# The border of two layers: layer 1's first weights split ahead of the residuals, the last group's tiles ended one by one, the root table loaded early

## Chip, cores and metric

The kernel runs on one core of a Trainium2 chip. A core has five engines with queues of their own that work side by side: TensorE (PE: matrix products, into PSUM), VectorE (DVE), ScalarE (ACT), GpSimd (POOL) and SyncE (SP, which here only issues loads). Each engine takes its instructions strictly in the order in which they were put in its queue, and waits at an instruction whose inputs are not there. The metric is the device time of one execution in microseconds (us), as the median of several.

## What is computed

Two layers of a diffusion backbone over 512 latent tokens with 256 context tokens, model width 1024, in fp32. Each layer is an attention block and a SwiGLU block, both with a modulated RMS norm ahead and a gated residual behind. Layer 0 mixes latent attention heads and neighbourhood heads, layer 1 has sliding-window heads. What matters here is the end of layer 0 and the start of layer 1:

```python
def swiglu(h, w_gate_up, w_down):
    g, u = jnp.split(h @ w_gate_up, 2, axis=-1)
    return (jax.nn.silu(g) * u) @ w_down

def modulate(x, shift, scale):
    return rms_norm(x) * (1 + scale) + shift
...
        h_lat = h_lat + g_f * swiglu(modulate(h_lat, sh_f, sc_f), ffn_w_gate_up[l], ffn_w_down[l])
        if ctx_out:
            h_ctx = h_ctx + cg_a * o_ctx
            h_ctx = h_ctx + cg_f * swiglu(modulate(h_ctx, csh_f, csc_f), ffn_w_gate_up[l], ffn_w_down[l])
...
def odd_mixer(a_lat, a_ctx, rows, cols, w_in, sinks, w_out, ctx_out):
...
    q, k, v = split(a_lat @ w_in, s)
```

So layer 1's first product (`a_lat @ w_in`) needs the norm of the whole residual stream, a sum of squares over all 1024 features of each token.

## The kernel before

**Numbers.** An fp32 operand is held as two parts, a rounded part and the rest, and a product is three matmuls (rounded by rounded, rounded by rest, rest by rounded; lines 320 to 322 in `mm3`, 1302 to 1304 in `product`). Splitting a loaded weight is a cast on ScalarE and a subtraction on VectorE: `load_w` (lines 307 and 308) for a 128x1024 weight panel, `parts` (lines 1289 and 1290) elsewhere. In the names of the trace, `wr` is a raw weight, `wh` and `wl`, `ph` and `pl`, or two tiles of `st` are its parts, `pss`, `pst`, `psd`, `pso` are PSUM banks (three, two, two and one of them). Activations stand with features on the partitions: eight feature tiles of 128, each with 512 latent columns (`LATS`) and 256 context columns (`CTXS`).

**The feed-forward.** `ffn` goes over the 22 inner tiles in groups (`CHUNKS`); layer 0's last group has the tiles 19, 20 and 21. Each is a `Pair` (gate and up tile at once, by a scheme of seven half-size products in place of eight): `head` (two products of 12 matmuls, "11" and "21"), `body` (T2, T3, T1), `tail` (22, T4), each on 384 columns. Between the products that share a bank, ScalarE copies the partial result out (lines 1341, 1348, 1351), and T1 cannot start before the copy of line 1348. The tail of a pair is written after the head of the next one. Its result is the product's second operand `hs`, in two halves of 384 columns, each a multiply (line 1360) and a split (lines 1289, 1290). Within a group the inner tiles are the contraction steps of the down product.

**The border.** After the last group `final0` adds the down product to the residual stream, tile by tile: `tile` (nine matmuls: three contraction steps of three), `residual` (VectorE, line 1166, then a square on ScalarE, line 1464), `add` (VectorE, line 1470: the running sum of squares). Seven latent tiles are written first; while they go, three weight panels of layer 1 (`first_w`: panels 8, 9, 0 of `w_in1`) are loaded and split. Then come the eighth latent tile, the context tiles (`C`, `RC`), and `normed`: 16 token sums on TensorE (line 1439), the root on ScalarE (line 1444), a reciprocal and four transposes. After that layer 1's products (`panels`) begin, between the remaining context tiles.

**What sets the order.** A scheduler orders each engine's instructions by data, by the order of the program and by a timeline of its own. Inside `in_order(...)` an engine keeps the program's order: before, that holds for VectorE from the first latent tile on, and for TensorE from the eighth on. Loads are issued by SP in one queue, each when its buffer is free; `wr` has three buffers, `nb` two, `rope` one. The `rope` buffer here takes the modulation weights of layer 1, one 512 KB load after the other, each used by one VectorE operation (line 215) and then replaced. The residuals of earlier groups lie in DRAM (`home`) and are fetched by POOL's queue.

Of the kernel before, what the change touches and what calls it, by code (L numbers as in the profile page):

```python
# [100 lines left out]
def hybrid_kernel(ctx: ExitStack, tc, I, out):  # L101
# [31 lines left out]
    def dma(o, i):  # L133
        return nc.sync.dma_start(f(o), f(i))
# [1039 lines left out]

    def kept_w(src, m):

        r = T("wr", [P, 384])
        dma(r, src(m))
# [127 lines left out]
    class Pair:  # L1306
# [38 lines left out]
        def body(self):  # L1345
# [3 lines left out]
            product(self.y, self.s3, self.ops["T3"], True)  # L1349
            product(self.z, self.s1, self.ops["T1"])  # L1350
# [3 lines left out]
        def tail(self):  # L1354
            product(self.z, self.s4, self.ops["22"])
# [3 lines left out]
            for c in (self.c2, self.c1) if self.w > NX else (slice(0, 2 * self.w),):  # L1359
                V.tensor_tensor(self.s[:, c], self.s[:, c], self.t[:, c], op=ALU.mult)  # L1360
                parts(self.s[:, c], *(x[:, c] for x in self.dst))

# [30 lines left out]
    def ffn(l, ops, sums, cs, tags, more, down, final):  # L1393

        for ci, (k0, kc) in enumerate(CHUNKS[l]):
            hs, last = [], None
            for j in range(k0, k0 + kc):
# [3 lines left out]
                elif j >= DIRECT[l]:  # L1401
# [4 lines left out]
                    if last:  # L1406
                        last.tail()
                    p.body()
# [14 lines left out]
    new = []  # L1423
# [22 lines left out]

    def final0(src, hs):
# [3 lines left out]
        ws = [ahead[0]] + [kept_w(src, m) for m in range(1, KT)]  # L1451
        sq, acc, ts, r = {}, {}, {}, {}
        more = (I["w_in1"][8], I["w_in1"][9], I["w_in1"][0])

        def tile(m, c, v):
            o = PG()
            o = o[:, : c.stop - c.start]
            mm3([(o, c)], ws[m], hs)
            return o
# [41 lines left out]
        def C(m):  # L1501
            ctx[m] = tile(m, CTXS, 1)
# [249 lines left out]
```

## Time and profile before

| what | us |
|---|---|
| median of three runs | 1618.03 |
| the three runs | 1613.65, 1618.28, 1618.03 |
| the profiled execution | 1612.09 |
| its span, first to last instruction | 1610.3 |
| TensorE busy in it | 1539.6 |
| VectorE busy in it | 1182.0 |
| mean granted TensorE clock | 0.986 |

A row of the trace's timeline is: start, duration, engine, line, operation, written tile <- read tiles, form, count; in brackets stands the engine's idle time before it and what ended it. A row of waits has the waiting engine, what it waited for, total, number of times and the longest. A row of stretches has the bounds, the length, then for PE, PE's weight loads, DVE, ACT and POOL the busy time (and number of instructions), the granted clock (1.00 is full), the DMA's busy share and GB/s. A row of a queue has packets, megabytes and its share; one of a load has its queue, the count, the size and the us from issue to landing. One feed-forward group of layer 0 ends, and the border lies, between about 940 and 1040 us of the span.

### The profile page before, as it was taken

The page shows a single profiled execution, that of the slowest core. Times are in us where ns is not written, and L with a number is a line of the kernel's source. Part 1 is how long each engine was busy: PE and PEld are TensorE (multiplying, and loading weights), DVE is VectorE, ACT ScalarE, POOL GpSimd, SP SyncE. Part 2 cuts the span into 40 slices and gives each one's busy share as a digit, 9 for nine tenths or more (in the row PEclk, how much of TensorE's full clock was granted, in tenths as well). Part 3 has the DMA queues.
Part 4 walks back from the last instruction along what each step waited for, and adds up shares of the span by engine and source line. Part 5 has one row for each costly group of instructions (what it writes and reads, how often), then busy time and mean ns, then how long its engine had stood idle before and what let it go on. Part 6 is the DMA issues. An engine that isn't in the chain of part 4 may idle for free.

```text
span 1610.3 us, 26632 instructions
## 1 busy us (share of the span) xinstructions
PE 1539.6 (96%) x10004; PEld 1375.9 (85%) x10004; DVE 1182.0 (73%) x2367; ACT 806.0 (50%) x1637; POOL 226.7 (14%) x219
## 2 busy tenths in 40 slices
PE   6999989999998999999999998999999999999997
PEld 4686877887988999998989997877889898899996
DVE  5495977577579687785867776768877688687686
ACT  5364587776455333342423244457756554454453
POOL 0152723230000000100000010283003000000000
PEclk9999999999998999999999999999999999999998
DMA  9445342004541465647565766121006133333322
GB/s 341 161 149 190 108 132 80 23 7 159 179 161 59 158 204 169 214 127 246 159 202 196 243 212 210 41 89 66 2 6 200 33 112 124 91 98 118 91 97 84
DMA packets 80465, 214.92 MB, mean 133 GB/s; under 512 B 10192, under 2 KB 17872, under 8 KB 80336
## 3 DMA queue, kind: packets, MB, share of 16 engines
q1 hardware_dynamic: 73552, 188.05, 36.5%
q0 software_dynamic: 4480, 22.02, 3.7%
q10 hardware_dynamic: 2304, 3.15, 0.5%
q8 instruction: 78, 1.28, 0.3%
q14 instruction: 51, 0.42, 0.1%
HBM read 186.97 MB, written 23.07 MB: 130 GB/s over the span
## 4 chain that ended last, share of the span: by engine, by line
PE 73%; DVE 12%; DMA 9%; issue 3%; ACT 2%; POOL 1%; SPq 0%; DVEq 0%; ACTq 0%
PE pso L532 5%; DMA rope<-in_mod_w_dram 4%; PE pss L320 4%; PE pss L321 4%; PE pss L322 4%; PE psd L320 3%; PE psd L321 3%; PE psd L322 3%; PE pss L1302 3%; PE pss L1304 3%; PE pss L1303 3%; PE psd L1304 3%; PE psd L1302 3%; PE psd L1303 3%; PE pst L479 2%
## 5 line engine op out<-in xcount | busy, mean ns | idle before, releaser
L307 ACT CAST wh<-wr 128x512 fp32r<-128x512 f32 (+2 forms) x142 | 108.4, 778 | 202.9 <-PE pss L321 43.3
L308 DVE TENSOR_TENSOR wl<-wr,wh 128x1024 fp32r<-128x1024 f32 (+2 forms) x139 | 127.1, 921 | 78.6 <-ACT wh L307 77.9
L538 ACT ACTIVATE p<-p,sm 128x512 f32<-128x512 f32 (+3 forms) x144 | 105.0, 730 | 26.3 <-DVE sm L542 24.0
L215 DVE CUSTOM_DVE_ANT_0 p<-rope,cond 128x1024 bf16<-128x1024 f32 x64 | 77.0, 1220 | 40.3 <-DMA rope<-in_mod_w_dram 40.1
L321 PE MATMUL psd<-b,wh 128*128 128x256 f32 (+4 forms) x257 | 87.7, 341 | 2.2 <-DVE b L1290 2.2
L1303 PE MATMUL pss<-b,wh 128*128 128x384 f32 (+1 forms) x270 | 84.0, 311 | 1.2 <-DVE b L345 1.2
L1302 PE MATMUL pss<-b,wh 128*128 128x384 f32 (+1 forms) x270 | 84.1, 311 | 0.7 <-ACT b L344 0.7
L1430 POOL DMA_DIRECT2D home<-p x40 | 21.6, 541 | 447.5 <-DVE p L1166 320.5
L1304 PE MATMUL pss<-b,wl 128*128 128x384 f32 (+1 forms) x270 | 83.9, 311 | 0.0
L320 PE MATMUL psd<-b,wh 128*128 128x512 f32 (+4 forms) x217 | 77.8, 358 | 2.1 <-ACT b L430 1.3
L320 PE MATMUL pss<-st,wh 128*128 128x256 f32 (+2 forms) x231 | 78.1, 339 | 0.4 <-ACT wh L307 0.4
L322 PE MATMUL pss<-st,wl 128*128 128x512 f32 (+2 forms) x231 | 77.8, 337 | 0.0
L532 PE MATMUL pso<-ph,b 128*64 128x256 f32 (+1 forms) x384 | 77.3, 359 | 0.3 <-DVE ph L470 0.2
L532 PE MATMUL pso<-pl,b 128*64 128x256 f32 (+1 forms) x384 | 76.8, 359 | 0.7 <-DVE pl L470 0.7
L322 PE MATMUL psd<-b,wl 128*128 128x512 f32 (+4 forms) x217 | 76.0, 351 | 0.0
L1304 PE MATMUL pst<-b,wl 128*128 128x384 f32 (+1 forms) x240 | 74.1, 310 | 0.6 <-DVE wl L1290 0.6
L1302 PE MATMUL pst<-b,wh 128*128 128x384 f32 (+1 forms) x240 | 74.5, 310 | 0.0
L1303 PE MATMUL pst<-b,wh 128*128 128x384 f32 (+1 forms) x240 | 74.5, 310 | 0.0
L321 PE MATMUL pss<-b,wh 128*128 128x256 f32 (+4 forms) x227 | 74.0, 327 | 0.1
L1289 ACT CAST wh<-ph 128x512 fp32r<-128x512 f32 x80 | 46.3, 620 | 43.8 <-PE pst L1303 14.6
L1302 PE MATMUL psd<-b,wh 128*128 128x384 f32 (+1 forms) x210 | 65.8, 313 | 0.0
L1304 PE MATMUL psd<-b,wl 128*128 128x384 f32 (+1 forms) x210 | 65.3, 313 | 0.5 <-DVE wl L1290 0.5
(606 smaller groups left out, 5385.0 us busy)
## 6 DMA issues: line engine op xcount, KB each, us to landing
wr<-in_w_gu_dram SPq DMA_DIRECT2D x88, 512.0 KB, 4.1
rope<-in_mod_w_dram SPq DMA_DIRECT2D x48, 512.0 KB, 3.5
wr<-in_w_out_dram SPq DMA_DIRECT2D x32, 512.0 KB, 3.6
wr<-in_w_dn_dram SPq DMA_DIRECT2D x64, 256.0 KB, 2.8
p<-home SPq DMA_DIRECT2D x40, 384.0 KB, 4.8
home<-p POOLq DMA_DIRECT2D x40, 384.0 KB, 4.5
wr<-in_w_in_dram SPq DMA_DIRECT2D x21, 512.0 KB, 4.0
st<-in_mod_wp_dram SPq DMA_DIRECT2D x32, 256.0 KB, 4.9
```

Source lines behind the costliest of these rows:

```text
L215: V.tensor_tensor_reduce(out=T("p", [P, D], mybir.dt.bfloat16), in0=w, in1=cond[:, v, :], op0=ALU.mult, op1=ALU.add, scale=1.0, scalar=0.0 ...
L307: S.copy(h, r)
L308: (G if eng else V).tensor_tensor(lo, r, f(h), op=ALU.subtract)
L320: PE.matmul(o, wh[:, k], mh[:, c], start=first and k == 0, stop=False)
L321: PE.matmul(o, wh[:, k], ml[:, c], start=False, stop=False)
L322: PE.matmul(o, wl[:, k], mh[:, c], start=False, stop=last and k == n - 1)
L532: ins = PE.matmul(o[64 * i : 64 * i + 64, c], v(kt), t, start=n == 0, stop=n == len(moving[i]) - 1)
L538: S.activation(p[:, c], p[:, c], AF.Exp, bias=nm, scale=-1.0, accum_out=dn)
L1289: S.copy(h, t)
L1302: PE.matmul(o, wh, xh, start=first and k == 0, stop=False, skip_group_check=not first)
L1303: PE.matmul(o, wh, xl, start=False, stop=False, skip_group_check=not first)
L1304: PE.matmul(o, wl, xh, start=False, stop=k == 3, skip_group_check=not first)
```

## The change

It touches the last group of layer 0's feed-forward and the border.

- The generator `ended` splits the last-but-one pair's tail in two, and `begin_border`, started at the last pair's head, fixes the order on TensorE and ScalarE from there (TensorE's until the border is done, ScalarE's until the last tail). It splits the down weights of tiles 0 and 1 and the layer 1 panel 8, starts tiles 0 and 1 on the first two contraction steps, then splits panel 9, and after the last tail panel 0.
- `final0` starts tiles 2, 3 and 4 on two steps as well (`started`), then all eight latent tiles go in order: tiles 0 to 4 need their third step only, 5 to 7 all three. All residuals come after the three splits of layer 1's weights.
- The raw down weights of tiles 2 to 7 go to the `nb` buffers, two to a buffer, in place of `wr`.
- A root of one column, whose result nothing reads, stands on ScalarE before the first residual; with it ScalarE's table for roots is loaded there.

```diff
+        if m < 2:
+            r = T("wr", [P, 384])
+        elif m % 2 == 0:
+            r = T("nb", [P, 768])
+            raw_w[:] = [r[:, 384:]]
+            r = r[:, :384]
+        else:
+            r = raw_w[0]
+        dma(r, src(m))
...
             product(self.y, self.s3, self.ops["T3"], True)
+            next(between, None)
             product(self.z, self.s1, self.ops["T1"])
...
-                    if last:
+                    if l == 0 and j == NFF - 1:
+                        between = begin_border(last, lambda m: I["w_dn"][l, m, :, k0 * P : (k0 + kc) * P], hs)
+                        next(between)
+                    elif last:
                         last.tail()
-                    p.body()
+                    p.body(between)
...
-            ahead.clear()
-            ahead[0] = kept_w(src, 0) if l == 0 and final and ci == len(CHUNKS[l]) - 1 else load_w(src(0), kc, P)
+            if l or ci < len(CHUNKS[l]) - 1:
+                ahead.clear()
+                ahead[0] = load_w(src(0), kc, P)
+            elif last:
+                next(between)
             if last:
                 last.tail()
+            next(between, None)
+            casts.close()
...
+    def lat_tile(m, w, hs, ks=(0, 3), o=None):
+
+        k = slice(*ks)
+        o = PG() if o is None else o
+        mm3([(o, LATS)], [x[:, k] for x in w], hs[k], ks[0] == 0, ks[1] == 3)
+        return o
+
+    def begin_border(last, src, hs):
+
+        fixed.enter_context(in_order(ON_PE))
+        casts.enter_context(in_order(ON_ACT))
+        tail = last.ended()
+        next(tail)
+        yield
+        for _ in tail:
+            pass
+        ahead.clear()
+        for m in range(2):
+            ahead[m] = kept_w(src, m)
+        first_w.append(load_w(I["w_in1"][8], KT, P))
+        yield
+        started.extend(lat_tile(m, ahead[m], hs, (0, 2)) for m in range(2))
+        first_w.append(load_w(I["w_in1"][9], KT, P))
+        yield
+        first_w.append(load_w(I["w_in1"][0], KT, P))
...
-        with in_order(ON_DVE):
-            for m in range(KT - 1):
-                residual(m, tile(m, LATS, 0), LATS, 0)
-                if m:
-                    add(m - 1, 0)
-                if m in (2, 4, 6):
-                    first_w.append(load_w(more[len(first_w)], KT, P))
-            with in_order(ON_PE):
-                residual(7, tile(7, LATS, 0), LATS, 0)
-                add(6, 0)
+        S.activation(T("sm", [P, 6, 2])[:, :1, 0], f(hs[2][0][:, :1]), AF.Sqrt, bias=eps, scale=0.0)
+        with fixed, in_order(ON_DVE):
+                started.extend(lat_tile(m, ws[m], hs, (0, 2)) for m in range(2, 5))
+                for m in range(KT):
+                    residual(m, lat_tile(m, ws[m], hs, *(((2, 3), started[m]) if m < 5 else ())), LATS, 0)
+                    if m:
+                        add(m - 1, 0)
```

How the instructions stand in the queues, at three places. A row has the line, the operation, the written tile <- the tiles read, and the shape. Line numbers of the changed kernel are higher, since lines were added.

VectorE, from the last split of the last pair's result on, before (line 308 is the split of a layer 1 panel, line 1166 a residual, line 1470 a sum of squares):

```order
L1290 TENSOR_TENSOR b_9695<-p_9728,b_9694 128x384
L1166 SCALAR_TENSOR_TENSOR b_9869<-psd_9931,mod_390_1879,b_9877 128x512
L1166 SCALAR_TENSOR_TENSOR b_9870<-pst_9944,mod_390_1879,b_9879 128x512
L1166 SCALAR_TENSOR_TENSOR b_9871<-pss_9957,mod_390_1879,b_9881 128x512
L1470 TENSOR_TENSOR p_9942<-p_9942,p_9955 128x512
L308 TENSOR_TENSOR wl_9974<-wr_9971,wh_9973 128x1024
L1166 SCALAR_TENSOR_TENSOR b_9872<-psd_9977,mod_390_1879,b_9883 128x512
L1470 TENSOR_TENSOR p_9942<-p_9942,p_9968 128x512
```

and now, from one row earlier in the same place:

```order
L1374 TENSOR_TENSOR p_9728<-p_9728,p_9729 128x384
L1299 TENSOR_TENSOR b_9695<-p_9728,b_9694 128x384
L308 TENSOR_TENSOR wl_9908<-wr_9905,wh_9907 128x1024
L1166 SCALAR_TENSOR_TENSOR b_9912<-psd_9853,mod_390_1879,b_9920 128x512
L1166 SCALAR_TENSOR_TENSOR b_9913<-pst_9860,mod_390_1879,b_9922 128x512
L1166 SCALAR_TENSOR_TENSOR b_9914<-pss_9967,mod_390_1879,b_9924 128x512
```

The third split of a layer 1 panel stands ahead of the first residual; the other two stand further ahead, between the steps of the last pair, and none is left among the residuals.

SP's queue, at the end of the last group, before (`wr` from `in_w_dn` is a raw down weight of 192 KB, `rope` from `in_mod_w` a modulation weight of 512 KB):

```order
L134 DMA rope_1935_9685<-in_mod_w_dram 128x1024
L134 DMA wr_9893<-in_w_dn_dram 128x384
L134 DMA wr_9899<-in_w_dn_dram 128x384
L134 DMA rope_1937_9689<-in_mod_w_dram 128x1024
L134 DMA rope_2076_10372<-in_rope_dram 128x1024
L134 DMA wr_9904<-in_w_dn_dram 128x384
```

and now:

```order
L134 DMA rope_1935_9685<-in_mod_w_dram 128x1024
L134 DMA wr_9829<-in_w_dn_dram 128x384
L134 DMA wr_9833<-in_w_in_dram 128x1024
L134 DMA rope_1937_9689<-in_mod_w_dram 128x1024
L134 DMA rope_2074_10374<-in_rope_dram 128x1024
L134 DMA wr_9867<-in_w_in_dram 128x1024
L134 DMA wr_9905<-in_w_in_dram 128x1024
```

The load just ahead of the last modulation weight is now layer 1's panel 8, of 512 KB, where a down weight of 192 KB stood.

ScalarE, around the last pair's products, now (line 1357 is the copy that T1 waits for, line 1361 the one that the product 22 waits for, line 1370 the activation behind 22):

```order
L1357 COPY p_9729<-pss_9730 128x384
L1298 CAST st_9544<-p_9578 128x384
L1298 CAST ph_9821<-wr_9823 128x384
L1298 CAST ph_9827<-wr_9829 128x384
L307 CAST wh_9835<-wr_9833 128x1024
L1298 CAST st_9936<-nb_9937 128x384
L1298 CAST st_9941<-nb_9937 128x384
L1298 CAST st_9945<-nb_9946 128x384
L1298 CAST st_9950<-nb_9946 128x384
L1361 COPY p_9729<-pss_9730 128x384
L307 CAST wh_9869<-wr_9867 128x1024
L1370 ACTIVATE p_9728<-pss_9730 128x384
```

and before:

```order
L1289 CAST st_9544<-p_9578 128x384 x2
L1348 COPY p_9729<-pss_9730 128x384
L1289 CAST st_9901<-wr_9899 128x384
L1289 CAST st_9906<-wr_9904 128x384
L1289 CAST st_9911<-wr_9909 128x384
L1351 COPY p_9729<-pss_9730 128x384
L1289 CAST st_9916<-wr_9914 128x384
L307 CAST wh_9973<-wr_9971 128x1024
L1356 ACTIVATE p_9728<-pss_9730 128x384
```

T1's copy now stands one cast of the pair before earlier, and between it and the copy of the product 22 stand all of the casts of six down weights and of the first layer 1 panel.

More of the change, by code (lines that the diff above doesn't have):

```diff
@@ L1173, in hybrid_kernel @@
     ahead = {}
+    raw_w = []
     def kept_w(src, m):
[L1177 to L1178 removed]
         if m < 2:
@@ L1354, in tail, with ended @@
         def tail(self):
+            for _ in self.ended():
+                pass
+        def ended(self):
             product(self.z, self.s4, self.ops["22"])
@@ L1395, in ffn @@
         for ci, (k0, kc) in enumerate(CHUNKS[l]):
-            hs, last = [], None
+            hs, last, between = [], None, iter(())
             for j in range(k0, k0 + kc):
@@ L1421, in ffn @@
                 final(src, hs)
-    new = []
+    new, fixed, casts = [], ExitStack(), ExitStack()
     def down0(m, w, hs):
@@ L1450, in final0, with tile @@
         old = [fetched(m, slice(0, NT), "b") for m in range(KT)]
-        ws = [ahead[0]] + [kept_w(src, m) for m in range(1, KT)]
+        ws = [ahead[m] if m < 2 else kept_w(src, m) for m in range(KT)]
         sq, acc, ts, r = {}, {}, {}, {}
[L1453 to L1458, printed above, removed]
+        def tile(m):
+            o = PG()[:, :NX]
+            mm3([(o, CTXS)], ws[m], hs)
             return o
@@ L1501, in C @@
         def C(m):
-            ctx[m] = tile(m, CTXS, 1)
+            ctx[m] = tile(m)
         def RC(m):
```

5 lines of the change are left out of this document (4 added, 1 removed).

## The prediction

> **What bounds the kernel now.** I read the page first, then TensorE's waits around the border of the layers, then that stage as a table of stretches, then the rows of single instructions.
>
> ```profile
> PE 1539.6 (96%) x10004; PEld 1375.9 (85%) x10004; DVE 1182.0 (73%) x2367; ACT 806.0 (50%) x1637; POOL 226.7 (14%) x219
> ...
> PE psd L1439 <- DVE p L1470: 5.6, 1, 5.6
> PE psd L320 <- ACT st L1289: 1.7, 1, 1.7
> ...
> 998.76:1004.32 5.56, 0.00 (x1) 0.00 (x0) 5.56 (x9) 1.82 (x3) 0.00 (x0) 0.72 0.92 280
> 1004.32:1010.53 6.21, 6.21 (x30) 6.21 (x30) 0.91 (x3) 2.43 (x5) 0.00 (x0) 0.50 0.48 143
> 1010.53:1016.37 5.84, 5.84 (x48) 5.84 (x47) 5.46 (x11) 3.09 (x6) 0.00 (x0) 0.92 0.00 0
> 1016.37:1036.00 19.63, 19.63 (x100) 16.36 (x98) 17.16 (x37) 10.56 (x20) 1.15 (x1) 1.00 0.00 1
> ```
>
> TensorE is busy for 96% of the span, so only what lets it wait, or slows its clock, has a price. The border has one large wait: for 5.56 us TensorE does nothing while VectorE is full (5.56 of 5.56). It costs twice, for in the next 6.21 us the granted clock is 0.50, and it is back at 1.00 only in the stretch after 1016.37. Which VectorE work is late, its rows say:
>
> ```profile
> 991.76 0.75 DVE L1166 SCALAR_TENSOR_TENSOR b<-psd,mod,b 128x512 f32<-128x512 f32 x1 [2.11 <-PE psd L322]
> ...
> 994.48 1.22 DVE L308 TENSOR_TENSOR wl<-wr,wh 128x1024 fp32r<-128x1024 f32 x1
> ...
> 1001.79 1.22 DVE L308 TENSOR_TENSOR wl<-wr,wh 128x1024 fp32r<-128x1024 f32 x1
> ...
> 1003.59 0.68 DVE L1470 TENSOR_TENSOR p<-p,p 128x512 f32<-128x512 f32 x1
> ```
>
> From the first residual (991.76) to the last sum (1004.27) VectorE has hardly a gap, and three of its operations are splits of layer 1's weights (the first and the last are shown, 1.22 each). At its pace, a little under the durations, they take 3 x 1.14 = 3.4 us, a residual 0.66 and a sum 0.60. TensorE had its last matmul before the wait at 998.48, after a border in this order:
>
> ```profile
> 983.28 0.34 PE L1302 MATMUL pss<-st,ph 128*128 128x384 f32 x1
> ...
> 985.38 0.39 PE L320 MATMUL pst<-st,st 128*128 128x512 f32 x1
> ...
> 994.36 0.39 PE L320 MATMUL psd<-st,st 128*128 128x512 f32 x1
> ...
> 996.45 0.29 PE L320 MATMUL pst<-st,ph 128*128 128x256 f32 x1
> ...
> 998.48 0.28 PE L322 MATMUL pss<-b,pl 128*128 128x256 f32 x1
> ```
>
> These rows give the three paces: 12 matmuls of 384 columns in 2.10 us (0.175 each), nine of 512 in 2.09 (0.232), 18 of 256 from 996.45 to 998.60 (0.119).
>
> **The change, part by part.**
>
> *Splits ahead of the residuals.* The changed order has all three before the first residual, so the chain from there is 8 residuals at 0.66 and 6 sums at 0.60, 8.9 us in place of 12.5. TensorE's own list is no shorter: tail product and last product of the final pair (24 x 0.175 = 4.2), first two contraction steps of tiles 2 to 4 (18 matmuls), third step of tiles 0 to 4 (15), tiles 5 to 7 (27), which is 60 x 0.231 = 13.9, two context tiles (2.1): 20.2 us. Tiles 5 to 7 now end one by one, so VectorE has caught up when tile 7 ends, as the context tiles begin. Residual 7 (0.66) and the sum behind it (0.60, with ScalarE's square beside it) take some 1.5 us with the hand-overs, the context tiles 2.1: the token sums' inputs come about 0.5 us early, and TensorE has no wait there. The 5.72 us from 998.60 to 1004.32 go; next late is TensorE itself.
>
> *The half clock goes with the wait.* At full clock the same operations stand later in the trace:
>
> ```profile
> 1024.76 0.95 PE L1439 MATMUL pss<-ones,p 128*128 128x1 f32 x8
> 1025.57 0.48 PE L758 MATMUL psd<-b,wh 128*128 128x512 f32 x1
> ...
> 1027.74 0.38 PE L449 MATMUL pso<-ident_r,sm 128*128 128x128 f32 x2
> 1027.88 0.47 PE L758 MATMUL psd<-b,wh 128*128 128x512 f32 x1
> ```
>
> Eight sums took 0.81, so 16 take 1.62; a context tile 9 x 0.119 = 1.07; four transposes 0.28. That is 2.97 for the stretch that took 6.21: 3.24 saved. The five context tiles behind it take 45 x 0.119 = 5.35 in place of 5.84: 0.49. Together 5.72 + 3.24 + 0.49 = **9.45 us** if TensorE comes to the context tiles when it did before.
>
> *Does it come there in time?* The last pair's product T1 now stands ahead of the first down tiles, and it needs the ScalarE copy of the product before it.
>
> ```profile
> 968.26 1.22 DVE L215 CUSTOM_DVE_ANT_0 p<-rope,cond 128x1024 bf16<-128x1024 f32 x1 [3.97 <-DMA rope<-in_mod_w_dram]
> ...
> 971.16 1.02 DVE L1290 TENSOR_TENSOR pl<-wr,ph 128x384 fp32r<-128x384 f32 x2
> ...
> 974.29 0.51 ACT L1289 CAST st<-p 128x384 fp32r<-128x384 f32 x1 [1.09 <-DVE p L1360]
> 974.71 0.47 ACT L1348 COPY p<-pss 128x384 f32<-128x384 f32 x1
> ...
> 974.85 0.50 PE L320 MATMUL psd<-st,ph 128*128 128x512 f32 x1 [1.67 <-ACT st L1289]
> ...
> 975.97 1.34 ACT L1289 CAST st<-wr 128x384 fp32r<-128x384 f32 x3 [0.79 <-PE pss L1303]
> ...
> 990.32 1.05 ACT L307 CAST wh<-wr 128x1024 fp32r<-128x1024 f32 x1 [1.26 <-DMA wr<-in_w_in_dram]
> ```
>
> The two splits at 971.16 move behind the tail of the pair before, so the multiply of that tail starts there; it takes 0.47, as each of them, the cast behind it 0.42, the copy 0.47, with 0.2 between engines: T1 starts at 972.7. Before, TensorE went idle at 974.85 - 1.67 = 973.18, and six matmuls of 512 columns (1.4) that then came first now stand behind T1: it is free at about 971.7. T1 ends at 974.8, and the 12 down matmuls at 977.6. The next product needs a copy that stands on ScalarE behind a tail's last cast (from 973.75, by the same paces), two casts, the weight's cast (1.05) and four casts (0.45 each): 978.25. From 978.35, 20.2 us end at 998.55, against 998.60 before. The old 1.67 us wait is traded for two smaller ones: zero, taken as between -1 and +1 us.
>
> *The load that gets in front.* All of this hangs on 968.26, where VectorE ended a 3.97 us wait for a 512 KB load. On SP's queue a 192 KB load went just before it; now a 512 KB load of layer 1's weight stands there.
>
> ```profile
> q0 software_dynamic: 362, 1.83, 64.1%
> q1 hardware_dynamic: 288, 0.72, 27.0%
> ...
> b<-home POOLq DMA_DIRECT2D x6, 384.0 KB, 6.7
> rope<-in_mod_w_dram SPq DMA_DIRECT2D x1, 512.0 KB, 5.8
> ...
> rope<-in_mod_w_dram SPq DMA_DIRECT2D x1, 512.0 KB, 3.4
> ...
> 967.00:968.00 1.00, 1.00 (x8) 1.00 (x7) 0.00 (x0) 0.00 (x0) 0.00 (x0) 1.00 1.05 434
> ...
> wr<-in_w_in_dram SPq DMA_DIRECT2D x3, 512.0 KB, 3.6
> ```
>
> The first four lines are from 962 to 970, where SP's queue (q1) shares the DMA with six residual loads on q0; the fifth is a load of the same size from 955 to 962, without them. The full DMA moves 434 GB/s. Alone the load took 3.4 us, of which its bytes are 1.2, so 2.2 pass without data; here 5.8 - 2.2 = 3.6 us went on 512 KB, 0.146 MB per us. The 320 KB more are 0.8 us if the DMA were theirs alone, **2.2 us** at the shared pace, and about 5 if the residual loads (6 x 384 KB) all went first. I take 2.2, the only one from this very load. T1 gets it in full: 974.9.
>
> The Trainium skill, "DMA: Bandwidth & Descriptors", section "Queues, rings and completion order", says that a DMA engine takes turns between its queues, a packet at a time. The trace agrees: 362 and 288 packets, near equal, for very unequal bytes. By that rule the added load moves at the shared pace, and the sum stays at 6.3 (below); with a DMA of its own, 0.8 late, it would be 8.65.
>
> TensorE then idles 971.7 to 974.9, 3.2 us. What such a gap does to the clock:
>
> ```profile
> 1254.91 0.38 PE L758 MATMUL pss<-b,wh 128*128 128x256 f32 x1 [2.82 <-ACT b L344]
> ...
> 1258.00:1260.00 2.00, 2.00 (x11) 2.00 (x11) 1.13 (x2) 0.32 (x1) 0.00 (x0) 0.50 0.03 8
> ```
>
> A 2.82 us gap in dense work was followed by half clock. I count a drop as likelier than not. With 3.5 us of half clock T1 ends at 978.75 in place of 977.0, the down matmuls at 981.5; without it the next product waits for its copy until 978.35 + 2.2 = 980.55 anyhow. So the late load costs 2.2, with the drop 3.15.
>
> The Trainium skill, "TensorE: Matmul & The Clock Gate", section "Why this matters for your kernels", advises no idle gaps over about 3 us. The 2.82 us gap with its 0.50 is a little under that. Taken strictly the rule has a gap of 2.2 + 1.0 us on its edge: with a drop 6.3 saved, without 7.25.
>
> *Edits that I cost at nothing.*
>
> ```profile
> 1005.58 1.28 ACT L1444 ACT_TABLE_LOAD   x1
> ...
> L542 DVE CUSTOM_DVE_ANT_0 p<-pss,nb x24: 677/685/692, 195.5 to 270.4; 128x512 f32<-128x512 f32 x24
> ...
> 273.40 0.33 SPq L134 DMA_DIRECT2D rope<-in_mod_w_dram  x1
> ```
>
> The root table's load (1.28) lay inside the half-clock sums; now it stands before the first square, while TensorE has third-step matmuls. If that cover went, 1.28. It must stand early, since faster sums would no longer hide it. The raw weights of tiles 2 to 5 are loaded to buffers that the attention bias leaves free at 271.1; SP's next load was issued at 273.40, so its queue isn't held. Tiles 6 and 7 load late, and their casts come behind the tail product's activation; that chain ends about 0.5 us before the third steps need it. The second layer 1 weight must land before that activation: 3.6 us after the first tile's split frees its buffer, which leaves about 1 us.
>
> **The rivals.**
>
> 1. *Late load and clock drop* (forecast): 9.45 - 3.15 = 6.3 us. Chance 0.42.
> 2. *Late load, no drop*: 7.25 us saved, 1610.8. Chance 0.20.
> 3. *Load in time*: delay under 1 us, 8.5 to 9.45 saved, 1609.1. For it: much of the load may move before the residual loads start. Chance 0.18.
> 4. *The gain is given back at the border*: the load 5 us late, drop included about 6 us; 3.5 us left, 1614.5. For it: the DMA was full for this whole window. Chance 0.15.
> 5. *Slower: attention of layer 1.* The scheduler has reordered transposes, scores and copies of its first head pairs, at some six places.
>
> ```profile
> PE pss L745 <- DVE sm L542: 1.7, 2, 1.2
> ```
>
> In the window of this wait the longest is 1.2 us. Six more would cost 7.2, which with the forecast's 6.3 saved ends 0.9 slower, 1618.9; it decides from six such waits on. Against it: nearly all reordered pieces stay within a few rows. Chance 0.05. That the change doesn't do what it says is ruled out by the order: the three splits stand ahead of the residuals.
>
> **How the numbers follow.** The profiled execution took 1612.09 us (span 1610.3), and 1612.09 - 6.3 = 1605.8. That execution lies 5.9 under the median shown, 1618.03, and the three runs reach from 1613.65 to 1618.28; I carry the saving to the median: **1611.7**. Range: the low end is the profiled execution less 9.45, 1602.6, rounded to 1603; the high end rival 4's 1614.5 and 1.5 for the spread of the runs, 1616; case 5 stays out. A measurement of this kernel can tell about 0.3% from no change, 4.9 us. Cases 1 to 3 (0.80) lie beyond it, of which I take off 0.05 for the spread of runs; rival 4 and most of rival 5 lie within it, and what is slower by more is a rival 5 with ten waits and more: faster 0.75, same 0.21, slower 0.04.
>
> **What would show it.** Right: no wait of TensorE ahead of the token sums; 16 sums in about 1.6 us at clock 1.00; the three splits before the first residual; sums starting between 998.5 and 1002. The late load shows as VectorE's wait for it ending near 970.5, a TensorE gap of about 3 us before T1, and a clock near 0.5 around 975 to 978. Wrong: a new wait before the residual's tiles (a split or cast behind a load), or a gap in attention that was not there.

## The result, and the profile after

| | before | after |
|---|---|---|
| median, us (10 runs each) | 1617.94 | 1606.88 |
| lowest to highest, us | 1613.65 to 1619.67 | 1603.78 to 1614.65 |
| profiled execution, us | 1612.09 | 1609.79 |
| its span, us | 1610.3 | 1608.0 |
| mean granted TensorE clock | 0.986 | 0.987 |

The ratio of the times is 0.9942, with a 95% interval of 0.9926 to 0.9958: 9.4 us of 1617.94, between 6.8 and 12.0. (The two medians alone lie 11.1 us apart.) All ratios here and below leave out three single executions that were disturbed (1706.91, 3850.43 and 7858.64 us, in three different kernels). The two profiled spans differ by 2.3 us only, and that is no contradiction. The profiles are two single executions, and the second one had lost time long before the change. The rows show the same token sums of an earlier norm, in the profile before and in the one after:

```profile
211.65 0.39 PE L924 MATMUL psd<-ones,b 128*128 128x1 f32 x3
```

```profile
215.30 0.28 PE L924 MATMUL psd<-ones,b 128*128 128x1 f32 x2
```

3.65 us are gone by these rows, where both kernels run the same instructions. In the second profile TensorE had just waited 2.16 us (to 209.36) and then ran at half clock; the first has no wait over 1.2 us there. So the change is read from the distance between two instructions that stand around it, the first product of pair 19 (the first pair of the last group) and the first product of layer 1's panels. TensorE's rows, before:

```profile
932.61 0.34 PE L1302 MATMUL pst<-b,wh 128*128 128x384 f32 x1
...
1016.37 0.40 PE L758 MATMUL psd<-b,wh 128*128 128x512 f32 x1
```

and after:

```profile
936.37 0.34 PE L1311 MATMUL pst<-b,wh 128*128 128x384 f32 x1
...
1012.67 0.40 PE L758 MATMUL psd<-b,wh 128*128 128x512 f32 x1
```

This **long stretch** took 83.76 us before and 76.30 after, 7.5 less. Most of the text uses a shorter one, the **border stretch**, from the first product of the last pair's T2 (967.61 before, 970.84 after) to the same end: 48.76 and 41.83, 6.9 less. TensorE's waits between 960 and 1110 us, after:

```profile
PE pss L1311 <- ACT p L1357: 2.1, 1, 2.1
PE pss L745 <- DVE sm L542: 1.9, 3, 1.2
```

The 5.6 us before the token sums and the 1.7 us before the first down tile are gone. A new wait of 2.1 us stands at T1, and the attention of layer 1 waits as it did (1.9 us in three waits, 1.7 in two before). The same part as a table of stretches, after:

```profile
975.20:977.31 2.11, 0.02 (x2) 0.01 (x1) 1.53 (x4) 1.21 (x3) 0.00 (x0) 1.00 0.76 262
978.00:980.87 2.87, 2.87 (x11) 2.87 (x9) 2.02 (x4) 2.31 (x5) 0.00 (x0) 0.50 0.00 0
980.87:1004.03 23.16, 23.16 (x115) 20.01 (x115) 19.28 (x30) 13.20 (x23) 0.00 (x0) 0.99 0.65 223
1004.03:1007.24 3.21, 3.21 (x31) 3.21 (x30) 0.67 (x2) 0.99 (x3) 0.00 (x0) 1.00 0.13 48
1007.24:1012.67 5.43, 5.43 (x48) 5.43 (x47) 5.15 (x11) 2.99 (x6) 0.00 (x0) 1.00 0.00 0
```

TensorE is idle before T1, then runs at half clock for 2.87 us (T1's last matmuls), and from 980.87 to the panels it has no gap and the full clock. The token sums start at 1004.03 without a wait, and the stretch from them to the next context tile takes 3.21 us at clock 1.00, where it took 6.21 at 0.50. Why T1 is late, rows of SP, VectorE and ScalarE show, after:

```profile
964.16 0.33 SPq L134 DMA_DIRECT2D wr<-in_w_in_dram  x1
965.30 0.33 SPq L134 DMA_DIRECT2D rope<-in_mod_w_dram  x1
...
972.88 1.23 DVE L215 CUSTOM_DVE_ANT_0 p<-rope,cond 128x1024 bf16<-128x1024 f32 x1 [5.73 <-DMA rope<-in_mod_w_dram]
...
976.78 0.47 ACT L1357 COPY p<-pss 128x384 f32<-128x384 f32 x1
...
991.94 1.23 DVE L308 TENSOR_TENSOR wl<-wr,wh 128x1024 fp32r<-128x1024 f32 x1 [0.39 <-ACT wh L307]
993.08 0.74 DVE L1166 SCALAR_TENSOR_TENSOR b<-psd,mod,b 128x512 f32<-128x512 f32 x1
...
1002.09 0.75 DVE L1166 SCALAR_TENSOR_TENSOR b<-psd,mod,b 128x512 f32<-128x512 f32 x1 [0.73 <-PE psd L322]
```

Panel 8's 512 KB go out 1.14 us ahead of the last modulation weights. VectorE's operation on these (its row at 972.88) begins 7.58 us after their issue (5.81 before), and the copy that T1 needs comes 3.9 us behind it. The last panel split stands right ahead of the first residual, and at the eighth residual it is VectorE that waits for TensorE (0.73): the chains have changed places.

### The profile page after: what moved, and what is told of

It is laid out like the page before. It is cut to its first block, busy times and chain, and to the rows that moved or that the text cites. A ratio compares the mean times of both kernels' runs of the same rounds, so it can differ in the third digit from the quotient of the medians.

```text
span 1608.0 us, 26628 instructions
## 1 busy us (share of the span) xinstructions
PE 1539.4 (96%) x10004; PEld 1375.2 (86%) x10004; DVE 1181.9 (74%) x2367; ACT 807.9 (50%) x1638; POOL 226.6 (14%) x219
## 3 DMA queue, kind: packets, MB, share of 16 engines
q10 hardware_dynamic: 2304, 3.15, 0.5%
q8 instruction: 78, 1.28, 0.3%
## 4 chain that ended last, share of the span: by engine, by line
PE 72%; DVE 13%; DMA 8%; issue 3%; ACT 2%; POOL 1%; DVEq 0%; SPq 0%; ACTq 0%
PE pso L532 5%; PE pss L320 4%; PE pss L321 3%; PE pss L322 3%; DMA rope<-in_mod_w_dram 3%; PE pss L1313 3%; PE pss L1312 3%; PE pss L1311 3%; PE psd L320 3%; PE psd L321 3%; PE psd L322 3%; DMA wr<-in_w_gu_dram 3%; PE psd L1313 3%; PE psd L1311 3%; PE psd L1312 3%
```

## The experiments

"Ahead" is what SP issued within 1.2 us ahead of the last modulation weights; in the three kernels with "none" a 192 KB load went 3.9 us ahead. "Landing" is the time from SP's issue of these weights to the VectorE operation on them, which waited for them in every profile. Ratios are to the kernel before, run on the same chip, with 95% intervals. All columns but the ratio come from one execution of each kernel. The two of one kernel differ by 0.5 and 0.85 us in the long stretch, and whether the clock halves behind a gap, which is worth some 1.4 us (half of the 2.87 us above), can differ from one execution to the next (last section). So differences of 1 or 2 us between single rows prove little.

| kernel | ahead of them on SP | residual loads, from that issue | landing | TensorE idle in the long stretch | long stretch | ratio |
|---|---|---|---|---|---|---|
| before | 192 KB | -0.49 | 5.81 | 7.9 | 83.76 | 1 |
| before, again | 192 KB | -0.07 | 5.05 | 6.5 | 82.91 | not timed |
| after | 512 KB | +0.05 | 7.58 | 2.7 | 76.30 | 0.9942 (0.9926 to 0.9958) |
| after, again | 512 KB | +1.50 | 4.49 | 2.2 | 75.84 | 0.9949 (0.9933 to 0.9966) |
| splits ahead, alone | 192 KB | -0.38 | 6.65 | 5.2 | 82.78 | 0.9984 (0.9971 to 0.9997) |
| splits back | 512 KB | -0.33 | 7.69 | 5.0 | 80.14 | 0.9982 (0.9962 to 1.0002) |
| whole tiles | 512 KB | -0.54 | 5.23 | 5.9 | 80.42 | 0.9997 (0.9984 to 1.0010) |
| no early table | 512 KB | +0.03 | 7.14 | 2.1 | 75.08 | 0.9958 (0.9943 to 0.9972) |
| tiles 0, 1 ahead of T1 | 512 KB | +0.06 | 7.48 | 4.8 | 78.83 | 0.9981 (0.9964 to 0.9998) |
| panel 8 held long | none | +9.00 | 3.49 | 5.6 | 79.80 | 0.9978 (0.9962 to 0.9994) |
| panel 8 behind, POOL | none | +2.11 | 3.37 | 0.6 | 72.94 | 0.9949 (0.9933 to 0.9965) |
| panel 8 behind, VectorE | none | -0.13 | 3.77 | 0.3 | 72.77 | 0.9924 (0.9908 to 0.9941) |
| residual loads held | 512 KB | +2.53 | 4.54 | 2.6 | 77.16 | 0.9931 (0.9915 to 0.9947) |

**One part alone.** The kernel before with the three splits moved, and nothing else:

```diff
+        first_w.extend(load_w(x, KT, P) for x in more)
         with in_order(ON_DVE):
...
-                if m in (2, 4, 6):
-                    first_w.append(load_w(more[len(first_w)], KT, P))
```

> The kernel before, with one part of the change alone: layer 1's three panel splits issued ahead of the residuals. Tiles, raw weights and root table stay as before. Border stretch 48.76 us before, 41.83 after. Theory A (the splits alone carry the gain): 3.7 us of splits leave the chain of residuals, the wait of 5.56 us before the token sums falls to about 1.9 us, with no half clock after it, and the stretch is 41.5 to 43.5. Theory B (the place alone is worth little, since the residuals cannot begin before the last pair's low part, and the splits then stand ahead of that or of the first residual): the wait stays above 4 us and the stretch above 46.

TensorE's waits in its border:

```profile
PE psd L1439 <- DVE p L1470: 2.2, 1, 2.2
PE psd L320 <- ACT st L1289: 1.9, 1, 1.9
PE psd L320 <- ACT b L1289: 0.3, 1, 0.3
PE psd L322 <- DVE pl L1290: 0.2, 1, 0.2
```

The wait before the sums fell from 5.6 to 2.2 us, near theory A's 1.9, but the clock still halved behind it, and a second half clock came behind the 1.9 us at the first down tile. The border stretch was 48.03 us, within theory B's range, the long one 0.6 under the mean of the two profiles before. Neither theory had both. VectorE's rows show what became of the splits:

```profile
997.46 1.22 DVE L308 TENSOR_TENSOR wl<-wr,wh 128x1024 fp32r<-128x1024 f32 x1
998.68 0.75 DVE L1166 SCALAR_TENSOR_TENSOR b<-psd,mod,b 128x512 f32<-128x512 f32 x1
```

The third split stands right ahead of the first residual, as theory B said, and that residual begins 26.95 us after T2 (998.68 less 971.73), where it was 24.15 before (991.76 less 967.61). TensorE's first down tile came 2.8 us later as well, in good part from the half clock behind its gap, which lies ahead of the moved splits. So part of the shorter wait is only a later TensorE, and this execution shows the splits as worth less than the times do: 0.9984 is 2.6 us (0.5 to 4.7).

**The other part alone.** The kernel after with the splits back among the residuals:

```diff
-        first_w.append(load_w(I["w_in1"][8], KT, P))
...
                     if m:
                         add(m - 1, 0)
+                    if m in (2, 4, 6):
+                        first_w.append(load_w(I["w_in1"][(8, 9, 0)[m // 2 - 1]], KT, P))
```

> The kernel after, with the three panel splits put back among the residuals (behind the residuals of tiles 2, 4 and 6, as before); tiles ended one by one, raw weights and root table stay as after. Border stretch 48.76 us before, 41.83 after. Theory A (the splits' place is what made the wait): three splits of 1.23 us on VectorE stand again in the chain of residuals, TensorE's wait before the token sums comes back with 3.0 to 5.0 us and the sums after it run at half clock; panel 8's load no longer stands ahead of the last modulation weights, so T1's gap is under 1 us. Stretch 43 to 46 us. Theory B (ending the tiles one by one lets the residuals start early enough, and the splits' place is of no account): the wait is under 1 us, and with the gap at T1 gone the stretch is 38.5 to 40.

```profile
PE pss L1311 <- ACT p L1357: 3.3, 1, 3.3
PE psd L1462 <- DVE p L1516: 1.4, 1, 1.4
```

These are its waits of TensorE. Before the sums 1.4 us came back, less than A's 3.0 and more than B's 1. The expectation had one thing wrong: panel 8's load was still issued first, since SP takes a load when its buffer is free (landing 7.69 us), and ScalarE's cast of that panel now stood ahead of T1's chain, so that the gap at T1 was 3.3. The border stretch, 46.09, is at the end of A's range, in part by luck: the wait before the sums was shorter than A has it and the gap at T1 longer.

**Whole tiles.** The kernel after with no tile begun ahead on two contraction steps:

```diff
-        started.extend(lat_tile(m, ahead[m], hs, (0, 2)) for m in range(2))
...
-                started.extend(lat_tile(m, ws[m], hs, (0, 2)) for m in range(2, 5))
...
-                    residual(m, lat_tile(m, ws[m], hs, *(((2, 3), started[m]) if m < 5 else ())), LATS, 0)
+                    residual(m, lat_tile(m, ws[m], hs), LATS, 0)
```

> The kernel after, with no down tile started ahead on two contraction steps: tiles 0 to 7 are computed whole, in order, behind T4 of the last pair; splits, raw weights and root table stay as after. Theory A (the tiles begun ahead are cover): TensorE has nothing to do while the last pair's parts are made (ScalarE and VectorE take some 5 us for them behind T4), nor while ScalarE copies T1's sum (product 22 waits 1 to 3 us); waits of 5 to 9 us appear in the place of the six tiles' two steps, and the stretch is 47 to 52 us. Theory B (residuals bound the stretch anyway): tiles begun ahead only wait later, and the stretch is 41 to 44.

```profile
PE pss L1311 <- ACT p L1361: 3.2, 1, 3.2
PE psd L320 <- ACT b L1298: 1.2, 1, 1.2
PE pss L1311 <- ACT p L1357: 0.3, 1, 0.3
```

The waits stand where A put them, at product 22 and at the first tile, and are shorter than it said (4.8 us in place of 5 to 9). The border stretch is 45.50, between the theories, and the long one 4.3 us over the kernel after. The tiles begun ahead are cover, worth 4.3 of the 7.3 us in the profiles. The times make them worth nearly the whole gain (0.9997, where the kernel after had 0.9949 on the same chip); that difference is open.

**No early table.** The dummy root is left out:

```diff
-        S.activation(T("sm", [P, 6, 2])[:, :1, 0], f(hs[2][0][:, :1]), AF.Sqrt, bias=eps, scale=0.0)
```

> The kernel after, without the dummy root of one column that loads ScalarE's root table ahead of the squares. Theory A (the table load stood on the way from the token sums to the spread, and C2 alone covers part of it): 1.28 us of table load between the sums and the root, of which the spread waits for 0.7 to 1.3 us more than now, stretch 42.4 to 43.2. Theory B (the load is made early anyway, or C2 covers it): stretch 41.5 to 42.1, no wait before the spread.

Rows of ScalarE and TensorE in it, at the root:

```profile
1001.25 1.28 ACT L1467 ACT_TABLE_LOAD   x1
1002.55 0.27 ACT L1467 ACTIVATE sm<-psd,eps 128x4 f32<-128x4 f32 x1
```

```profile
1002.78 0.28 PE L322 MATMUL pss<-b,st 128*128 128x256 f32 x1
1003.08 0.65 PE L449 MATMUL pso<-ident_r,sm 128*128 128x128 f32 x4
```

The load stands between the squares and the root, and the spread still follows the context tile C2: 3.04 us after the sums began, where it was 2.86 after. So the early table is worth 0.2 us by this distance, which is B's answer: C2 covers the rest. The times show no loss either (0.9958 beside 0.9949). The border stretch (40.99) is below B's range, because the gap at T1 was 1.67 us and the clock did not halve.

**The kernels again.** Both unchanged, profiled once more:

> The kernel after, unchanged, profiled once more. Theory A (the gain is what the border stretch shows): the stretch from the last pair's T2 to the first panel product comes out at 41.3 to 42.4 us again (48.76 before), with T1's gap near 2.1 us and half clock behind it, and the run 6 to 8 us shorter than before. Theory B (the gap at T1 is an accident of one execution): another execution has a gap under 1 us and a stretch of 38.5 to 40, which would explain a timed gain of 9 us or more.

> The kernel before, unchanged, profiled once more. Theory A (its border does not hang on when the loads land, as its T1 has two down tiles ahead of it and the wait before the token sums ends the stretch): stretch within 0.7 us of 48.76. Theory B (it varies from execution to execution as that of the kernel after does, by some 4 us): 45 to 47 us or above 50.

Before, the border stretch came out at 48.39 with the same 5.6 us wait: A. After, it came out at 37.91, without a gap at T1, which looks like B. The rows of that execution show why it is not that simple:

```profile
PE pst L1313 <- DVE wl L1299: 2.0, 1, 2.0
```

```profile
977.53 0.48 ACT L1357 COPY p<-pss 128x384 f32<-128x384 f32 x1 [0.82 <-PE pss L1313]
```

The first is a wait of TensorE in pair 19's products (at 949, with half clock behind it), and the second the copy for T1, which here waits for TensorE. Two things made room. TensorE, which had stood still earlier, began T2 6.99 us after the issue of the modulation weights, where it was 5.54 in the other execution. And the weights landed in 4.49 us in place of 7.58, with the residual loads 1.5 us behind them; this is the larger part. Even so the long stretch is 75.84, within 0.5 of the other execution, since it holds the earlier wait as well. Hence it is the steadier measure of the two.

**The load that got in front.** Three kernels put panel 8's load behind the last modulation weights. A one-column copy into the raw tile, which the load then overwrites, makes the load wait for a value; they differ in that value and in the engine of the copy. The first, with `hold` the copy after T2:

```diff
         r = T("wr", [P, kt * m])
+        hold is None or G.tensor_copy(r[:, :1], hold)
         dma(r, src)
...
-        first_w.append(load_w(I["w_in1"][8], KT, P))
+        first_w.append(load_w(I["w_in1"][8], KT, P, hold=p.t[:, :1]))
```

> The kernel after, with the load of panel 8's raw weights held back until the last pair's copy after T2 is made (a one-column copy on POOL into the raw tile, which the load then overwrites; nothing else is computed differently). The measure is the border stretch: from the first product of the last pair's T2 on TensorE to the first product of layer 1's panels, 48.76 us in the profile before (967.61 to 1016.37) and 41.83 after (970.84 to 1012.67). Theory A (the late load): the 512 KB load ahead of the last modulation weights delays these by some 1.8 us, and through VectorE and ScalarE T1; without it they land in about 5.8 us again where they took 7.6, T1's gap of 2.09 us shrinks to 0.3 or less, no half clock follows, and the stretch is 38.2 to 39.0. Theory B (the gap is that of T1 moved ahead of the down tiles, whatever the load does): the six home loads fill the queues anyway, the landing stays at 7 us or more, the gap at 1.7 to 2.1 us, and the stretch at 41.3 to 42.3. Against the kernel after, A gives a run shorter by 2.8 to 3.6 us, B no difference.

A's first half held: landing 3.49 us, no gap at T1. But then the loads of panels 8, 9 and 0, those of tiles 6 and 7's weights and eight residual loads all went out between 971.7 and 976.3. Tile 6's weights were 11.2 us under way (975.18 to 986.42; 4.2 after), ScalarE stood still for 4.0 us before their cast with the last pair's cast behind it, and TensorE got one wait in place of the other:

```profile
PE psd L320 <- ACT b L1298: 4.6, 1, 4.6
```

The second takes a value that exists 7 us earlier (`hold=last.t[:, HT : HT + 1]`):

> The kernel after with two loads changed in order: panel 8's raw weights are loaded behind the last modulation weights instead of ahead of them (a one-column copy on POOL, of a value that exists by then, into the raw tile that the load overwrites; nothing else is computed differently, and all other loads keep their places). Border stretch 41.83 us after; in the run that held this load until T2's copy, T1's gap was gone and the modulation weights had landed 3.5 us after their issue, but the loads behind came late. Theory A (the queue is served in order, and the 512 KB ahead were the delay): the modulation weights land in 3.5 to 5 us, T1 starts without a gap, panel 8 lands early enough for its cast, no later wait appears, and the stretch is 38.2 to 39.2 us, 2.6 to 3.6 under the kernel after. Theory B (loads issued within a microsecond or two share the engines whatever their order): the modulation weights land 5.5 to 7 us after issue, half a microsecond to 1.5 us of the gap stay, and the stretch is 39.5 to 41.5.

Landing 3.37 and border stretch 39.12, within A's range, with 0.6 us of wait at the third steps. The times do not show it: 0.9949, the same as the kernel after on that chip. And POOL's copy had also put the residual loads, which POOL issues in order, 2.1 us behind the weights. So a third kernel makes the copy on VectorE (`V.tensor_copy`, `hold=f(hs[0][1][:, :1])`), and a fourth leaves panel 8 in front and holds the residual loads instead:

```diff
-        t = B(tag=tag)
+        t = B(tag=tag); hold is None or G.tensor_copy(t[:, :1], hold)
...
-        old = [fetched(m, slice(0, NT), "b") for m in range(KT)]
+        old = [fetched(m, slice(0, NT), "b", f(hs[0][1][:, :1]) if m == 2 else None) for m in range(KT)]
```

> The kernel after, with panel 8's load behind the last modulation weights, as in the run w8_behind, but released by a one-column copy on VectorE, so that POOL and the six loads of residual tiles that it issues (2.36 MB) keep their time; in w8_behind POOL's copy had put these 2.1 us behind the modulation weights. Theory A (the six loads of residual tiles are what the modulation weights wait beside): issued within 0.5 us of these, they keep the landing at 5.2 to 6.7 us, as in the profile before and in the run with the splits alone (5.8 and 6.7 us, with no panel load ahead), T1's gap is 0.3 to 1.5 us, stretch 38.5 to 40. Theory B (panel 8's load is the delay): landing 3.4 to 4.5 us, no gap, stretch 37.9 to 38.5.

> The kernel after, with panel 8's load ahead of the last modulation weights as it is there, and the six loads of residual tiles put some 1.5 to 2.5 us behind these (a one-column copy on POOL of a value made by then, into one of the tiles that the loads overwrite). Theory A (the six loads are the contention): the modulation weights land 4 to 5 us after issue where they took 7.6, T1's gap is 0 to 0.5 us, stretch 37.9 to 39. Theory B (panel 8's load is the delay): landing 6.5 to 7.6 us, gap 1.3 to 2.1 us, stretch 40.5 to 42.

SP, POOL and VectorE with panel 8 behind, copy on VectorE:

```profile
964.10 0.33 SPq L134 DMA_DIRECT2D rope<-in_mod_w_dram  x1
966.20 0.33 SPq L134 DMA_DIRECT2D wr<-in_w_in_dram  x1
...
963.97 3.23 POOL L1170 DMA_DIRECT2D b<-home  x6 [23.06 <-PE pst L1313]
...
967.87 1.23 DVE L215 CUSTOM_DVE_ANT_0 p<-rope,cond 128x1024 bf16<-128x1024 f32 x1 [1.73 <-DMA rope<-in_mod_w_dram]
```

and with the residual loads held:

```profile
961.98 0.33 SPq L134 DMA_DIRECT2D rope<-in_mod_w_dram  x1
...
964.51 3.23 POOL L1170 DMA_DIRECT2D b<-home  x6 [0.35 <-issue]
...
966.52 1.23 DVE L215 CUSTOM_DVE_ANT_0 p<-rope,cond 128x1024 bf16<-128x1024 f32 x1 [2.70 <-DMA rope<-in_mod_w_dram]
```

Both expectations had the two causes as alternatives, and each run answers for itself: with the residual loads beside it and panel 8 behind, the landing is 3.77 us (B of the one); with panel 8 ahead and the residual loads later, 4.54 (A of the other). Either alone costs 0.4 to 1.1 us over the 3.4 us with neither; both together make 7.1 to 7.7 in four of five profiles (5.23 in the fifth). With the residual loads held, ScalarE later waited 3.4 us for panel 9's weights and 1.7 us for tile 6's, and TensorE 1.7 us at the third steps with half clock behind it: the long stretch is 77.16, and why those loads came late in that execution is not shown. The kernel with panel 8 behind has 0.3 us of wait left in the long stretch, 72.77 us, 3.3 under the mean of the two profiles after. Its ratio, 0.9924, is the lowest; its interval still meets that of the kernel after, and the kernel with the residual loads held, whose stretches miss its expectation (border 42.49) and lie over the kernel after's, was timed at 0.9931. So the profiles show it ahead, and the times do not settle it.

**Filling the gap.** Tiles 0 and 1 begun ahead of T1 in place of behind it:

```diff
         first_w.append(load_w(I["w_in1"][8], KT, P))
-        yield
         started.extend(lat_tile(m, ahead[m], hs, (0, 2)) for m in range(2))
+        yield
```

> The kernel after, with the two steps of down tiles 0 and 1 (12 products) put ahead of the last pair's T1, in the place where TensorE waits 2.09 us. Border stretch 41.83 us after. Theory A (the gap and its half clock are simply filled): both go, 2.09 us and some 1.5 us, stretch 38.2 to 39. Theory B (the wait moves): the product 22 that follows T1 needs the copy of T1's sum, which ScalarE makes in its written order only behind the cast of panel 8 and four casts of down weights (at 982.41 in the profile after); TensorE then waits 2.5 to 3.5 us there, the clock halves there, and the stretch is 40.8 to 41.8.

It ran at 0.9981 of before, slower than the kernel after. The profile is from another execution of the same kernel, which took 1611.38 us.

> The same kernel as e4_tiles_first (tiles 0 and 1 begun ahead of T1), once more for its profile. Its time was 0.9981 of before, which puts the stretch at 45 to 46 us. Theory A (the wait moved): no gap at T1, and a wait of 2.5 to 4 us at product 22 for the copy of T1's sum, with half clock behind it; stretch 41 to 43. Theory B (tiles 0 and 1 themselves wait for the last pair but one's parts, ahead of T1): a wait of 3 to 6 us at tile 0 and a second one at product 22; stretch 43 to 46.

```profile
PE psd L320 <- ACT ph L1298: 4.2, 1, 4.2
PE pss L1311 <- ACT p L1361: 0.6, 1, 0.6
```

The waits are B's, 4.2 us at tile 0 and a short one at 22, and the border stretch is 44.86. Both theories of the first expectation had it lower, with no wait ahead of T1. The cause is not the parts of the pair before, as B has it: tile 0 waits for the cast of its own weights (`ph`), which ScalarE makes behind T1's copy. In the kernel after, the gap at T1 is only 2.1 us because T1 is the first to need that late chain; whatever needs more of it waits longer.

## Why the prediction held, point by point

The time after, 1606.88 us, lies in the range of 1603 to 1616, 4.8 under the forecast's 1611.7. The forecast of 6.3 us saved is too small against the timed 9.4 (6.8 to 12.0), and within the interval of a second timing, 8.2 (5.5 to 10.8). By the times alone rival 3, with 8.5 to 9.45 saved, fits better; only the profiles show that the late load and the half clock were there. Against them the forecast is near: 6.9 us in the border stretch of the first two, and 7.3 in the long one as means of two profiles each (83.34 less 76.07).

- *The wait before the token sums and its half clock.* Right: 5.56 us to nothing. The stretch behind it was forecast as 2.97 + 5.35 = 8.32 us and took 3.21 + 5.43 = 8.64. TensorE's list from product 22 to the sums was forecast as 20.2 us and took 20.19 (983.84 to 1004.03).
- *Splits ahead of the residuals.* The step credited two things together: the splits' place, and tiles that end one by one. The profiles show that it takes both: 2.2 us of wait stay with the first alone, 1.4 with the second alone, and with either the clock falls again behind the wait.
- *The late load.* The mechanism is shown: with panel 8's load behind, the landing falls to 3.4 to 3.8 us and the gap at T1 is gone. Its size against before, forecast as 2.2 us, was 1.8 (7.58 less 5.81). What the step missed is that the kernel before was already late: its three profiles with 192 KB right ahead have 5.05 to 6.65 us, where nothing right ahead and the same residual loads beside gave 3.77.
- *Gap, half clock and their 3.15 us.* Mis-sized. The gap was 2.09 us where 3.2 were forecast, the half clock some 2.9 where 3.5 were. The down tiles behind T1 ended 13.0 us after T2 began (983.84 less 970.84), forecast 13.9 (981.5 less 967.61), or 10.74 without the late load (978.35): it cost 2.3, not 3.15. These 0.9 us, less 0.3 from the slower sums and context tiles, are nearly the whole difference to the border stretch's 6.9. That the clock would drop was read from one row of 2.82 us, which is not a single gap (last section).
- *The gap as a constant.* The forecast gave one size to it. Its size depends on when TensorE gets there and on how long the load takes, 7.58 us in one execution and 4.49 in the other. Rival 3 (load in time) is what the second profile shows at the border, beside an earlier wait. What makes the timed gain larger than 7.3 us stays open; both intervals reach down to it.
- *The edits at nothing.* The early table was worth 0.2 us, not the 1.28 that was named if its cover went: the context tile between sums and spread covers it even at full clock, so "it must stand early" was wrong. SP's queue was not held by the early raw weights: the next modulation load went out at 276.35, 2.95 us later than before, in an execution that had lost 3.65 by then. The late casts of tiles 6 and 7 cost nothing in the kernel after, and 0.3 to 4.6 us in the kernels that moved loads.
- *The other rivals.* No loss in layer 1's attention: from the panels to the next norm's sums it took 208.72 us before (1016.37 to 1225.09) and 208.43 after (1012.67 to 1221.10):

```profile
1225.09 0.39 PE L365 MATMUL pst<-ones,p 128*128 128x1 f32 x3
```

```profile
1221.10 0.39 PE L365 MATMUL pst<-ones,p 128*128 128x1 f32 x3
```

## What to carry to other kernels

Moving work off a chain pays only until the next chain is the longer one: look for the second wait before crediting the first, since here the halves of the change alone gave 0.6 and 3.2 us of the 7.3 in the profiles, and 2.6 and 2.9 of 8 to 9 in the times (the second of these is not clear of nothing: -0.3 to 6.1). When work is moved forward its loads go forward too, and in an in-order queue they stand ahead of a load that something is waiting for; putting the one behind the other took the gap away and was worth some 3 us more in two profiles, which the times have not confirmed. To see a few microseconds in single profiles, measure between two fixed instructions that stand well outside the change, not the span and not the nearest wait, and take more than one execution of each kernel before believing 1 or 2 us.

## What the runs showed of the hardware

**The clock can halve after shorter gaps than the prediction's row, and the length alone does not decide.** That row had 2.82 us, and it was not a single gap. TensorE's work resumed at 1254.91, and a second wait followed before the clock fell:

```profile
1256.34 0.39 PE L759 MATMUL pss<-b,wh 128*128 128x256 f32 x1 [0.81 <-DVE b L345]
```

Around the border, gaps of up to 1.67 us between full-width matmuls left the clock alone, and gaps of 1.72, 1.89, 2.09, 3.3 and 4.6 us brought half clock. Two stretches behind such a gap (before, behind 1.67 us; residual loads held, behind 1.72):

```profile
974.85:977.50 2.65, 2.65 (x14) 2.56 (x15) 1.52 (x4) 1.67 (x4) 0.00 (x0) 1.00 0.08 28
```

```profile
988.50:991.00 2.50, 2.50 (x8) 1.92 (x7) 1.91 (x3) 1.84 (x4) 0.00 (x0) 0.50 0.41 64
```

That is no threshold, though. Elsewhere in the same profiles the same wait, at the same instruction of an earlier part and nearly equally long, went both ways (first residual loads held, then panel 8 behind with POOL's copy):

```profile
825.15 0.39 PE L321 MATMUL psd<-b,wh 128*128 128x256 f32 x1 [2.15 <-DVE b L1299]
...
825.15:828.00 2.85, 2.85 (x17) 2.76 (x18) 2.04 (x5) 0.51 (x1) 0.00 (x0) 1.00 0.75 218
```

```profile
827.67 0.58 PE L321 MATMUL psd<-b,wh 128*128 128x256 f32 x1 [2.17 <-DVE b L1299]
...
827.67:830.67 3.00, 3.00 (x10) 2.81 (x11) 2.21 (x5) 0.51 (x1) 0.00 (x0) 0.50 0.74 223
```

In the latter profile a gap of only 1.31 us (to 245.38) also brought half clock, some 2 us after work resumed; in the kernel after it came 0.7 us after T1's gap, and in the row at 827.67 at once. What decides besides the length no run here shows. The Trainium skill, "TensorE: Matmul & The Clock Gate", section "Why this matters for your kernels", advises against gaps over about 3 us. Here 1.31 to 2.17 us were enough in some executions, and the measurement decides.

**Whether sums of one column keep the clock up is not shown.** In the kernel with the splits back, a gap of 1.45 us and 1.8 us of token sums at clock 1.00 were followed by 0.62:

```profile
1001.20:1003.00 1.80, 1.76 (x16) 1.77 (x16) 0.77 (x2) 0.85 (x3) 0.00 (x0) 1.00 0.96 233
1003.00:1005.00 2.00, 2.00 (x13) 2.00 (x13) 0.18 (x1) 0.27 (x1) 0.00 (x0) 0.62 0.67 266
```

The gap alone may have done it, as the one of 1.31 us did without such sums behind it. In the kernel after the same sums, with no gap ahead of them, were followed by clock 1.00 (1007.24 to 1012.67).
